# Reciprocals on another DMA queue, output chunks loaded two ahead, and the last block's closing steps behind later chunks, in a hybrid attention layer on one Trainium2 core

## The chip, the cores and the metric

The kernel runs on one core of one Trainium2 chip. The metric is device time in microseconds (us) of one execution. A core has TensorE (PE: matmuls, with PEld for its weight loads), VectorE (DVE), ScalarE (ACT), GpSimd (POOL) and SyncE (SP), each with an instruction queue of its own that it works through in order, and 16 DMA engines. Here SP issues nearly all DMAs. Three runs of the kernel before gave 1417.75 us in the median, 1410.29 to 1420.25.

## The reference

One encoder layer on 2048 positions of width 1024: an input projection, a gated linear attention over 512 of the columns, a softmax attention with 4 heads over the others, and one output projection with a residual and a LayerNorm. Only the last two stages bear on the change:

```python
    def attend(blk):
        qn, qr = blk
        s = (jnp.einsum('bqhd,bkhd->bhqk', qn, k_nope) + jnp.einsum('bqhr,bkr->bhqk', qr, k_r))
        p = jax.nn.softmax(s, axis=-1)
        return jnp.einsum('bhqk,bkhv->bqhv', p.astype(v.dtype), v)
...
    return jnp.concatenate([o_a, o_b], axis=-1) @ w_out
...
        x = layer_norm(DEEPNORM_ALPHA * x + mixed, ln_g[layer], ln_b[layer])
```

## The kernel before

Everything is float32. A matmul operand is split into a high part (`hi`, a copy to float32r on ACT, L115) and the rest (`lo`, a subtraction on DVE or POOL, L121), and a product is three matmuls (`mm3`, L147 to L149: high by high, low by high, high by low).

**Attention.** 16 blocks (4 heads by 4 groups of 512 queries). A block's scores come in 8 groups j of 256 keys: ten matmuls into a PSUM tile pS of two banks, of which there are two (L998 to L1002); `copy` on ACT takes it to a score tile s (L1007), `smax` on DVE keeps a running maximum (L1020). From the maxima come transposes on PE (mx, mb), then per group `sub` on DVE, `exp` on ACT, the split `phi` (ACT) and `plo` (POOL), the product `pv` with the values into a tile o, and the sums `acc`. The closing steps of a block are `tot` and `tsum` (the sums, transposed on PE into a tile sx in the bank pX), `rcp` (DVE: reduction L1108, reciprocal L1109, then the DMA of L1110 that stores 512 reciprocals to r_s in DRAM), `oh` and `ol` (split of o), `y` (the product with the value weights, into the bank pX) and `yc` (ACT copy, and the DMA of L1133 to ob_s). The queries of a later block are fetched by SP (L984, L988).

**Order.** All steps of the 16 blocks, and of the first four output chunks, are given a number, their place, in the tables PLACE, PLACE_LAST (for the last block) and PLACE_OUT. A place counts score groups: 8 to a block. `put` collects the steps; they are issued sorted by place, and `in_order` chains each engine's instructions, SP's too, in just this order. What comes behind that list (L1206 on) is ordered by the framework's scheduler, which goes by its own estimate of when each instruction is ready, and by program order where several are.

**Output chunks.** 16 chunks c of 128 positions. `load` (L1271) brings `of` (L1278: the linear attention's part; L1281: ob_s) and `gr` (L1279: the gates gm_s; L1280: the reciprocals r_s, broadcast). Both tiles come from the pool xf, which has two buffers in all. `gate` on POOL multiplies the second half of of by both parts of gr (L1287, twice), `hi` and `lo` split the halves. `product` is 48 matmuls per chunk, 24 for each half of the output columns, with `residual` on DVE after each half (L1331, then statistics L1332); even chunks write to the single banks pM and pX (pmb, px), odd ones to one tile of two banks (po). `finish` is the LayerNorm: L1344 to L1347, then `rsqrt` with Ln and Exp on ACT (L158, L159) and small DVE steps (L160 to L163), L1350, and two stores on SP (L1351). The rows of the output weights come by `fetch_w` (L1253) and are split into tiles woh and wol. `prepare(c)` loads and splits a chunk and loads its rows of x (xr, L1300). Chunks 0 to 3 are interleaved with the last block; for the others `prepare(c + 1)` stands ahead of chunk c's product. The last block's closing steps stand behind the finish of chunk 3.

Of the kernel before, what the change touches and what calls it, by code (L numbers as in the profile page):

```python
# [37 lines left out]
LATE_GATES = (NCH - 1, NCH - 2, 0)  # L38
STORE_POOL = (0, 1)
ENGINES = tuple(getattr(mybir.EngineType, n) for n in ("PE", "Activation", "DVE", "Pool", "SP"))  # L40
RND = 1.5 * 2.0 ** 23


# [28 lines left out]
PLACE_LAST = dict(  # L72
    sub=(9.1, 8.5, 8.63, 6.24, 10.95, 10.71, 7.9, 9.69),
    exp=(9.8, 11.1, 11.03, 11.51, 15.26, 10.75, 19.78, 16.58),
    hi=(11.57, 11.59, 12.49, 12.47, 16.56, 18.98, 23.59, 33.63),
    lo=(12.92, 14.95, 16.42, 18.28, 22.53, 23.3, 25.08, 34.29),
    pv=(15.43, 16.41, 17.68, 23.59, 30.52, 30.14, 33.06, 37.83),
    acc=(14.17, 13.67, 13.91, 12.97, 17.46, 24.17, 28.21, 33.8),
)


PRE_W, PRE_BLOCK = 4, 9
PLACE_OUT = dict(
    hi0=(-24.43, -15.24, -7.79, 34.96),
    lo0=(-21.2, -13.14, -5.7, 45.1),
    gate=(-19.0, -12.69, -4.28, 45.77),
    hi1=(-17.8, -11.53, 1.93, 46.3),
    lo1=(-16.64, -10.48, 17.64, 46.35),
    pre_hi=1.44,
    pre_lo=4.06,  # L90
    w_hi=0.11,
    w_step=5.72,
    w_lo=2.87,
    part=(0.52, 0.83, 3.02, 6.31, 9.13, 17.89, 18.98, 27.0),
    whole=(25.32, 49.8),
    sum=(41.6, 53.01),
)


# [7 lines left out]
class K:  # L107
# [20 lines left out]
        return s  # L128

    @contextmanager  # L130
    def in_order(self, last):


        traced = self.nc.cur_bb.bb.instructions
        end = traced[-1]
        yield
        n = next(k for k in reversed(range(len(traced))) if traced[k] is end) + 1
        for i in traced[n:]:
            if i.engine in ENGINES:
# [824 lines left out]
    def attention(self):  # L964
# [4 lines left out]
        with ExitStack() as ctx:  # L969
# [132 lines left out]

            def rcp(i):

                h, b = blocks[i]
                d = stt[i]
                rc = bp.tile([P, 4], F32, tag="rc", name=f"rc{i}")
                V.tensor_reduce(rc, d["x"], AX.X, ALU.add)  # L1108
                V.reciprocal(rc, rc)  # L1109
                nc.sync.dma_start(self.r_s[b][:, h].rearrange("o (e p) -> p (o e)", p=P), rc)  # L1110

            def oh(i):
                d = stt[i]
# [36 lines left out]
            def put(place, fn, *a):  # L1150
                todo.append((place, len(todo), fn, a))
# [5 lines left out]
            own = (("tot", tot), ("tsum", tsum), ("rcp", rcp), ("oh", oh), ("ol", ol), ("y", y), ("yc", yc))  # L1157
            for i in range(nb):
                for j in range(NP):
                    t = NP * i + j  # L1160
# [13 lines left out]
            for k in range(NK):  # L1174
                if k < PRE_W:
                    v = NP * (PRE_BLOCK + k)
                    hi, lo = v + out["pre_hi"], v + out["pre_lo"]
                else:
                    hi = end + out["w_hi"] + (k - PRE_W) * out["w_step"]
                    lo = hi + out["w_lo"]  # L1180
                if k == 0:
                    put(hi - 6, op.fetch_w, k)
                put(hi, op.split_hi, k)
                put(lo, op.split_lo, k)
                if k + 1 < NK:
                    put(lo + 0.01, op.fetch_w, k + 1)
                put(end + out["part"][k], lambda k: [op.part(o, k) for o in first[:2]], k)
            for c, o in enumerate(first):
                put(end + (out["lo1"][c - 1] + 0.01 if c else out["hi0"][0] - 6), op.load, o)
# [13 lines left out]
                    fn(*a)  # L1203
            ends = [i for e, i in last.items() if e not in (mybir.EngineType.PE, mybir.EngineType.DVE)]

            def prepare(c):  # L1206
                o = dict(c=c)
                with self.after(*ends):
                    op.load(o)
                    op.hi(o, 0)  # L1210
                    op.lo(o, 0)
                    op.gate(o)
                    op.hi(o, 1)
                    op.lo(o, 1)
                op.load_res(o)
                return o

            for o in first[:2]:
                op.finish(o)
            nxt = prepare(4)  # L1220
            for o in first[2:]:
                op.load_res(o)
                op.residual(o, 0)
                op.residual(o, 1)
                op.finish(o)
            with self.after(*last.values()):
                for _, f in own:
                    f(nb - 1)
            for c in range(4, NCH):
                o = nxt  # L1230
                if c < NCH - 1:
                    nxt = prepare(c + 1)
                op.product(o)
                op.finish(o)


class OutProj:
# [3 lines left out]
    def __init__(self, kern, ctx, qp, bp, sp, ps, pa, pb):  # L1241
        self.k, self.nc, self.qp, self.bp, self.sp, self.ps = kern, kern.nc, qp, bp, sp, ps
        self.single = (pa, "mb"), (pb, "x")
        self.sm = ctx.enter_context(kern.tc.tile_pool(name="smo", bufs=2, reuse_waits="tile"))
        self.raw, self.W = {}, {}
        self.ln = None

    def slot(self, name, dt=F32):
        return self.sp.tile([P, 2, 512], dt, tag="s", name=name)
# [15 lines left out]
    def split_lo(self, k):  # L1265
# [2 lines left out]
        self.k.lo(wl, self.raw[k], wh, "pool")  # L1268
        self.W[k] = wh, wl

    def load(self, o):  # L1271
# [9 lines left out]
        nc.sync.dma_start(of[:, 1], kern.ob_s[b][:, :, cs])  # L1281
        o["oh"], o["ol"] = [], []
# [51 lines left out]
    def finish(self, o):  # L1334
        kern, nc, sm = self.k, self.nc, self.sm
        V, Ac = nc.vector, nc.scalar
        c, rr = o["c"], o["rr"]
        if self.ln is None:
            self.ln = [self.slot(n) for n in ("lng", "lnb")]
            for t, n in zip(self.ln, ("ln_g", "ln_b")):  # L1340
                nc.sync.dma_start(t, kern.ins[n].rearrange("p (a d) -> p a d", a=2))
# [78 lines left out]
```

## Time and profile before

| What | us |
|---|---|
| median of three runs | 1417.75 |
| the profiled execution | 1418.9 |
| its span | 1417.1 |
| TensorE busy | 1318.7 |
| VectorE busy | 1006.3 |
| ScalarE busy | 823.6 |
| GpSimd busy | 730.1 |

Times in the profile are counted from the span's start. The projections and the linear attention take about the first half, attention reaches to about 1200 us, and the output chunks fill the rest, chunks 0 to 3 partly inside the last block. A timeline row gives start, duration, engine, line, operation, output from input, count, and in brackets the idle time of that engine just before, with what ended it. The chain of waits gives start, duration and what it was. Groups give busy time, mean ns and idle time. Matmuls are pipelined, so that one of 512 columns is shown as 0.39 us while the next starts 0.23 us later.

### The profile page before, as it was taken

The numbers are of one execution on the slowest core, as the hardware profiler recorded it, in microseconds if no ns is written. First come the engines' busy times: TensorE is split into PE (matmuls) and PEld (weight loads), VectorE is DVE, ScalarE is ACT, GpSimd is POOL, SyncE is SP. The second block draws the span as 40 slices with busy tenths as digits, with TensorE's granted clock in tenths as the row PEclk, the third lists the DMA queues.
The fourth block names the chain that finished last, engine by engine and source line by source line (L and its number), as shares of the span: only waits on it lengthen the run. The fifth ranks groups of instructions, "written<-read, shape, count | busy, mean of one in ns | idle before, by whom it ended". The sixth has DMA issues, their size and how long they took to land.

```text
span 1417.1 us, 19889 instructions
## 1 busy us (share of the span) xinstructions
PE 1318.7 (93%) x7056; PEld 1142.1 (81%) x7056; DVE 1006.3 (71%) x1829; ACT 823.6 (58%) x1353; POOL 730.1 (52%) x394
## 2 busy tenths in 40 slices
PE   6899999999989998899999999999999998966997
PEld 6899899998879888889788888888888776745785
DVE  7657754545687777776788888888888785564565
ACT  6555556555666555555688877888888685211100
POOL 3432423232332332330288888888899896634520
PEclk9899999999999999999999999999999999988999
DMA  7222223131655555544502332433332203565541
GB/s 248 75 67 69 72 62 108 53 86 57 208 196 172 171 172 161 183 154 135 156 1 38 45 43 45 64 46 66 52 82 38 68 15 43 197 159 176 176 158 45
DMA packets 108916, 147.39 MB, mean 104 GB/s; under 512 B 17838, under 2 KB 63278, under 8 KB 108816
## 3 DMA queue, kind: packets, MB, share of 16 engines
q1 hardware_dynamic: 108144, 144.02, 37.4%
q0 software_dynamic: 672, 2.10, 0.4%
q8 instruction: 56, 0.92, 0.3%
q14 instruction: 44, 0.36, 0.1%
HBM read 94.93 MB, written 51.15 MB: 103 GB/s over the span
## 4 chain that ended last, share of the span: by engine, by line
PE 46%; issue 6%; DVE 6%; DMA 6%; POOL 4%; ACT 4%; SPq 0%; DVEq 0%; POOLq 0%; ACTq 0%
PE o L148 4%; PE o L149 4%; PE o L147 4%; PE pS L998 4%; PE pS L1001 4%; PE pS L999 4%; PE pS L1000 4%; PE pS L1002 4%; DMA gr<-gm_s 2%; POOL of L1287 2%; PE po L147 1%; PE po L148 1%; PE po L149 1%; PE ipm L147 1%; DVE MMb L121 1%
## 5 line engine op out<-in xcount | busy, mean ns | idle before, releaser
L121 POOL TENSOR_TENSOR pl<-s,ph 128x1024 fp32r<-128x1024 f32 x128 | 306.2, 2410 | 61.3 <-ACT ph L115 46.7
L1020 DVE TENSOR_TENSOR rm<-pS,rm 128x512 f32<-128x512 f32 x210 | 144.5, 688 | 48.1 <-ACT s L1007 44.5
L1007 ACT ACTIVATE s<-pS 128x1024 f32<-128x1024 f32 x128 | 131.2, 1025 | 68.6 <-PE pS L1002 54.5
L1044 DVE TENSOR_TENSOR s<-s,mb 128x1024 f32<-128x1024 f32 x128 | 151.2, 1213 | 8.6 <-PE mb L1038 8.4
L115 ACT ACTIVATE ph<-s 128x1024 fp32r<-128x1024 f32 x128 | 133.8, 1058 | 26.8 <-PE o L149 26.1
L147 PE MATMUL ipa<-wah,xah 128*128 128x384 f32 (+1 forms) x384 | 131.6, 343 | 6.6 <-ACT wah L115 6.6
L1048 ACT ACTIVATE s<-s 128x1024 f32<-128x1024 f32 x128 | 132.7, 1049 | 8.3 <-DVE s L1044 6.0
L149 PE MATMUL ipa<-wah,xal 128*128 128x384 f32 (+1 forms) x384 | 126.7, 330 | 0.0
L148 PE MATMUL ipa<-wal,xah 128*128 128x384 f32 (+1 forms) x384 | 126.0, 328 | 0.0
L643 POOL TENSOR_TENSOR Us<-Us,cw 128x512 f32<-128x512 f32 x16 | 18.2, 1137 | 202.2 <-DVE Us L640 172.9
L998 PE MATMUL pS<-qh,ckvT_h 128*128 128x512 f32 x256 | 103.1, 403 | 1.9 <-ACT s L1007 1.3
L147 PE MATMUL o<-ph,vh 128*128 128x512 f32 x256 | 103.7, 405 | 0.1
L148 PE MATMUL o<-pl,vh 128*128 128x512 f32 x256 | 101.6, 397 | 1.9 <-POOL pl L121 1.9
L149 PE MATMUL o<-ph,vl 128*128 128x512 f32 x256 | 101.7, 397 | 0.0
L1001 PE MATMUL pS<-rh,krs 128*128 128x512 f32 x256 | 101.2, 395 | 0.0
L1000 PE MATMUL pS<-qh,ckvT_l 128*128 128x512 f32 x256 | 101.0, 395 | 0.0
L999 PE MATMUL pS<-ql,ckvT_h 128*128 128x512 f32 x256 | 101.0, 394 | 0.0
L1002 PE MATMUL pS<-rl,krs 128*128 128x512 f32 x256 | 100.8, 394 | 0.0
L1071 DVE TENSOR_TENSOR ap<-ap,s 128x512 f32<-128x512 f32 x120 | 83.5, 696 | 16.9 <-ACT s L1048 14.3
L115 ACT ACTIVATE oh<-of 128x512 fp32r<-128x512 f32 x32 | 20.2, 630 | 125.2 <-POOL of L1287 90.3
L147 PE MATMUL po<-woh,oh 128*128 128x512 f32 x144 | 59.7, 415 | 30.9 <-DVE rr L1331 27.8
L147 PEld LDWEIGHTS ipa<-wah,xah 128*128 128x128 f32 x384 | 74.3, 193 | 7.3 <-ACT wah L115 6.6
(319 smaller groups left out, 3938.0 us busy)
## 6 DMA issues: line engine op xcount, KB each, us to landing
xcf<-xT_dram SPq DMA_DIRECT2D x16, 512.0 KB, 4.6
xr<-x_dram SPq DMA_DIRECT2D x16, 512.0 KB
out_dram<-rr SPq DMA_DIRECT2D x32, 256.0 KB, 3.3
xaf<-xT_dram SPq DMA_DIRECT2D x14, 512.0 KB, 4.3
SU<-su_s SPq DMA_DIRECT2D x16, 256.0 KB, 4.5
qdb<-qd_s SPq DMA_DIRECT2D x16, 256.0 KB, 5.4
oib<-oi_s SPq DMA_DIRECT2D x16, 256.0 KB, 3.2
ub<-u_s SPq DMA_DIRECT2D x16, 256.0 KB, 3.5
```

The costliest lines, as they stand in the source:

```text
L115: return nc.scalar.activation(dst, src, AF.Copy).ins
L121: return e.tensor_tensor(dst, src, hi.bitcast(F32), ALU.subtract).ins
L147: mm(out, ah, bh, start=start, stop=False)
L148: mm(out, ah, bl, start=False, stop=False)
L149: mm(out, al, bh, start=False, stop=stop)
L998: mm(ps[:, e], kh, qh, start=True, stop=False)
L999: mm(ps[:, e], kh, ql, start=False, stop=False)
L1000: mm(ps[:, e], kl, qh, start=False, stop=False)
L1001: mm(ps[:, e], kr, rh, start=False, stop=False)
L1002: mm(ps[:, e], kr, rl, start=False, stop=True)
L1020: V.tensor_tensor(d["rm"], src[:, e], d["rm"], ALU.max)
L1044: V.tensor_tensor(s, s, d["mb"][:, None, :].to_broadcast([P, 2, QB]), ALU.subtract)
```

## The change

- `rcp` no longer issues a DMA. A new step `keep`, with a place of its own, issues the store of the reciprocals, now from ACT instead of SP.
- From chunk 4 on gr comes not from xf but from two tiles of the pool of score tiles, kept for even and odd chunks; xf then holds only the of tiles of these chunks.
- `load` and the split are taken apart: in chunk c's turn chunk c+2 is loaded and chunk c+1 is split. SP's instructions behind the list are chained in program order (`sp_order`).
- The last block's closing steps move from behind chunk 3's finish to behind the finishes of chunks 4 (tot, tsum), 5 (rcp, keep, oh, ol), 6 (y) and 7 (yc).
- The LayerNorm's two vectors are loaded in the list (`load_ln`), behind the split of the last weight rows, instead of at the first finish.
- All places are new.

```diff
 PLACE = dict(
-    copy=0.66,
-    max=0.98,
-    sub=(8.99, 8.91, 7.08, 8.85, 7.8, 5.4, 8.0, 7.24),
-    exp=(9.53, 10.02, 8.65, 9.56, 9.46, 9.27, 9.15, 8.24),
-    hi=(10.62, 10.59, 10.16, 10.6, 10.11, 10.96, 9.97, 10.3),
-    lo=(11.09, 12.25, 12.38, 11.97, 11.89, 11.89, 11.05, 10.44),
-    pv=(12.27, 12.73, 12.77, 12.49, 12.61, 12.3, 12.63, 11.92),
-    acc=(12.22, 11.24, 11.05, 0, 10.8, 11.32, 9.98, 9.11),
-    acc0=11.5,
-    tmax=1.41,
-    rmax=1.66,
-    bmax=1.67,
-    tot=10.0,
-    tsum=13.05,
-    rcp=15.73,
-    oh=12.61,
-    ol=12.89,
-    y=16.44,
-    yc=16.75,
+    copy=0.73,
+    max=1.21,
+    sub=(9.47, 8.65, 7.39, 7.37, 7.49, 6.63, 6.95, 7.44),
+    exp=(10.18, 9.95, 7.63, 9.15, 8.26, 9.12, 7.84, 8.01),
+    hi=(10.39, 10.41, 9.81, 10.32, 9.82, 10.74, 10.53, 10.47),
+    lo=(11.99, 11.22, 11.21, 12.62, 11.98, 11.51, 10.87, 10.63),
+    pv=(12.35, 12.1, 11.89, 12.65, 12.27, 12.25, 12.14, 11.45),
+    acc=(12.45, 11.78, 12.32, 0, 10.57, 11.24, 10.03, 9.22),
+    acc0=10.78,
+    tmax=1.26,
+    rmax=1.27,
+    bmax=1.48,
+    tot=11.2,
+    tsum=12.04,
+    rcp=13.55,
+    keep=14.21,
+    oh=12.34,
+    ol=12.99,
+    y=16.55,
+    yc=16.9,
 )
...
             def rcp(i):
-                h, b = blocks[i]
                 d = stt[i]
                 rc = bp.tile([P, 4], F32, tag="rc", name=f"rc{i}")
                 V.tensor_reduce(rc, d["x"], AX.X, ALU.add)
                 V.reciprocal(rc, rc)
-                nc.sync.dma_start(self.r_s[b][:, h].rearrange("o (e p) -> p (o e)", p=P), rc)
+                d["rc"] = rc
+
+            def keep(i):
+                h, b = blocks[i]
+                Ac.dma_start(self.r_s[b][:, h].rearrange("o (e p) -> p (o e)", p=P), stt[i]["rc"])
...
                 if k + 1 < NK:
                     put(lo + 0.01, op.fetch_w, k + 1)
+                else:
+                    put(max(lo, end + 26) + 0.02, op.load_ln)
...
-            def prepare(c):
-                o = dict(c=c)
-                with self.after(*ends):
-                    op.load(o)
-                    op.hi(o, 0)
-                    op.lo(o, 0)
-                    op.gate(o)
-                    op.hi(o, 1)
-                    op.lo(o, 1)
-                op.load_res(o)
-                return o
-
-            for o in first[:2]:
-                op.finish(o)
-            nxt = prepare(4)
-            for o in first[2:]:
-                op.load_res(o)
-                op.residual(o, 0)
-                op.residual(o, 1)
-                op.finish(o)
-            with self.after(*last.values()):
-                for _, f in own:
-                    f(nb - 1)
+            late = dict(last)
+            sp_order = lambda: self.in_order(late, SP_ONLY)
+            rest = {c: o for c, o in enumerate(first)}
+
+            def load(c):
+                if c < NCH:
+                    rest[c] = dict(c=c)
+                    op.load(rest[c])
+
+            def split(c):
+                if c < NCH:
+                    with self.after(*ends):
+                        for j in range(2):
+                            op.hi(rest[c], j)
+                            op.lo(rest[c], j)
+                            if j == 0:
+                                op.gate(rest[c])
+
+            with sp_order():
+                load(4)
+                for c in (2, 3):
+                    op.load_res(rest[c])
+                load(5)
+                for c in (0, 1):
+                    op.finish(rest[c])
+                split(4)
+                op.load_res(rest[4])
+                for c in (2, 3):
+                    op.residual(rest[c], 0)
+                    op.residual(rest[c], 1)
+                    op.finish(rest[c])
             for c in range(4, NCH):
-                o = nxt
-                if c < NCH - 1:
-                    nxt = prepare(c + 1)
-                op.product(o)
-                op.finish(o)
+                with sp_order():
+                    load(c + 2)
+                    split(c + 1)
+                    if c + 1 < NCH:
+                        op.load_res(rest[c + 1])
+                    op.product(rest[c])
+                    op.finish(rest[c])
+                with self.after(*last.values()), sp_order():
+                    for f in {4: (tot, tsum), 5: (rcp, keep, oh, ol), 6: (y,), 7: (yc,)}.get(c, ()):
+                        f(nb - 1)
...
-        gr = o["gr"] = kern.xfp.tile([P, 2, 4, P], F32, tag="xf", name=f"gr{c}")
+        if c < 4:
+            gr = kern.xfp.tile([P, 2, 4, P], F32, tag="xf", name=f"gr{c}")
+        else:
+            gr = self.gr[c % 2] = self.gr.get(c % 2) or self.slot(f"gr{c}").rearrange("p a (b d) -> p a b d", b=4)
+        o["gr"] = gr
```

The tables PLACE_LAST and PLACE_OUT have the same keys as before and new numbers.

More of the change, by code (lines that the diff above doesn't have):

```diff
@@ L40 @@
 ENGINES = tuple(getattr(mybir.EngineType, n) for n in ("PE", "Activation", "DVE", "Pool", "SP"))
+SP_ONLY = ENGINES[-1:]
 RND = 1.5 * 2.0 ** 23
@@ L51 @@
 PLACE = dict(
[L52 to L70 removed]
+    copy=0.73,
[18 more added lines that the diff above has]
+    yc=16.9,
 )
 PLACE_LAST = dict(
[L73 to L78, printed above, removed]
+    sub=(9.67, 8.74, 8.38, 6.77, 10.45, 3.53, 9.53, 5.55),
+    exp=(10.14, 9.35, 10.49, 8.31, 13.01, 14.59, 17.1, 18.05),
+    hi=(10.43, 11.83, 12.21, 14.39, 15.18, 22.96, 28.7, 34.03),
+    lo=(15.35, 16.07, 20.38, 20.41, 24.45, 25.82, 33.5, 36.25),
+    pv=(16.29, 16.53, 21.45, 24.62, 26.22, 30.32, 41.89, 43.83),
+    acc=(11.54, 13.81, 13.58, 13.82, 21.36, 25.57, 30.56, 39.92),
 )
@@ L83 @@
 PLACE_OUT = dict(
[L84 to L96, printed above, removed]
+    hi0=(-26.0, -16.05, -6.97, 34.17),
+    lo0=(-23.84, -12.96, -6.1, 40.96),
+    gate=(-20.72, -12.46, -4.41, 43.92),
+    hi1=(-19.28, -11.15, 1.03, 47.74),
+    lo1=(-16.82, -9.22, 22.19, 48.77),
+    pre_hi=1.22,
+    pre_lo=3.57,
+    w_hi=0.74,
+    w_step=6.49,
+    w_lo=4.26,
+    part=(1.05, 2.03, 5.45, 8.05, 10.24, 17.37, 21.96, 27.24),
+    whole=(24.99, 55.73),
+    sum=(38.16, 49.19),
 )
@@ L130, in in_order @@
     @contextmanager
-    def in_order(self, last):
+    def in_order(self, last, engines=None):
         traced = self.nc.cur_bb.bb.instructions
@@ L138, in in_order @@
         for i in traced[n:]:
-            if i.engine in ENGINES:
+            if i.engine in (engines or ENGINES):
                 if i.engine in last:
@@ L1155, in at @@
                 return p[j] if isinstance(p, tuple) else p
-            own = (("tot", tot), ("tsum", tsum), ("rcp", rcp), ("oh", oh), ("ol", ol), ("y", y), ("yc", yc))
+            own = (("tot", tot), ("tsum", tsum), ("rcp", rcp), ("keep", keep), ("oh", oh), ("ol", ol), ("y", y), ("yc", yc))
             for i in range(nb):
@@ L1269, in split_lo, with load_ln @@
         self.W[k] = wh, wl
+    def load_ln(self):
+        self.ln = [self.slot(n) for n in ("lng", "lnb")]
+        for t, n in zip(self.ln, ("ln_g", "ln_b")):
+            self.nc.sync.dma_start(t, self.k.ins[n].rearrange("p (a d) -> p a d", a=2))
     def load(self, o):
@@ L1337, in finish @@
         c, rr = o["c"], o["rr"]
[L1338 to L1341, printed above, removed]
         mv = sm.tile([P, 2], F32, tag="mv", name=f"mv{c}")
```

3 lines of the change are left out of this document (1 added, 2 removed).

## The prediction

> **What bounds the kernel now.** I read the page first, its busy times and slices; then a table of windows to see where TensorE is not full; then each engine's timeline in those windows, and SyncE's queue.
>
> ```profile
> PE 1318.7 (93%) x7056; PEld 1142.1 (81%) x7056; DVE 1006.3 (71%) x1829; ACT 823.6 (58%) x1353; POOL 730.1 (52%) x394
> 1000.00:1100.00 100.00, 100.00 (x451) 81.28 (x450) 84.36 (x115) 82.37 (x91) 91.83 (x42) 1.00 0.34 61
> 1180.00:1237.00 57.00, 52.22 (x221) 41.86 (x220) 29.80 (x48) 21.14 (x28) 36.64 (x20) 0.94 0.52 141
> 1237.00:1250.00 13.00, 8.77 (x34) 6.80 (x33) 12.83 (x27) 1.04 (x3) 4.40 (x3) 0.87 0.60 202
> 1250.00:1337.00 87.00, 59.96 (x245) 48.06 (x243) 45.52 (x80) 12.37 (x29) 40.26 (x30) 0.86 0.57 159
> 1337.00:1409.00 72.00, 70.76 (x308) 57.51 (x308) 40.35 (x87) 5.37 (x17) 15.72 (x12) 1.00 0.36 119
> ```
>
> In the window rows the columns are length, busy time (count) of PE, PEld, DVE, ACT and POOL, granted clock, DMA share and GB/s. Attention is bound by TensorE: 100 us busy in 100. So are the last output chunks, 70.76 in 72. Between them TensorE has holes, 4.2 us in 13 and 27 in 87, and the granted clock falls to 0.86: what it does run there runs partly at half speed. The timeline of PE names the holes; the bracket is the idle time before the row and what ended it.
>
> ```profile
> 1200.30 0.79 PE L147 MATMUL po<-woh,oh 128*128 128x512 f32 x1 [3.08 <-ACT woh L115]
> 1202.79 0.79 PE L148 MATMUL po<-wol,oh 128*128 128x512 f32 x1 [1.70 <-POOL wol L121]
> 1240.19 1.12 PE L1101 MATMUL sx<-ident,acc 128*128 128x128 f32 x4 [2.93 <-DVE rr L1331]
> 1249.63 0.50 PE L147 MATMUL y<-ofh,wv_h 128*128 128x512 f32 x1 [1.30 <-DVE u L1345]
> 1274.64 0.80 PE L147 MATMUL po<-woh,oh 128*128 128x512 f32 x1 [11.46 <-DVE rr L1331]
> 1310.46 0.80 PE L147 MATMUL po<-woh,oh 128*128 128x512 f32 x1 [13.29 <-DVE rr L1331]
> 1337.06 0.50 PE L147 MATMUL po<-woh,oh 128*128 128x512 f32 x1 [2.31 <-DVE rr L1331]
> 1402.87 0.50 PE L147 MATMUL po<-woh,oh 128*128 128x512 f32 x1 [0.78 <-DVE rr L1331]
> ```
>
> The hole of 11.46 us, followed backwards through ACT, POOL, DVE and SP:
>
> ```profile
> 1253.69 0.45 SPq L1133 DMA_DIRECT2D ob_s<-yc  x1
> 1254.66 0.52 SPq L1281 DMA_DIRECT2D of<-ob_s  x1
> 1267.35 2.60 POOL L1287 TENSOR_TENSOR of<-of,gr 128x512 f32<-128x512 f32 x2 [11.38 <-DMA of<-ob_s]
> 1269.98 0.63 ACT L115 ACTIVATE oh<-of 128x512 fp32r<-128x512 f32 x1 [15.66 <-POOL of L1287]
> 1270.52 0.19 ACT L158 ACTIVATE ln_l<-u 128x1 f32<-128x1 f32 x1
> 1270.97 0.99 DVE L160 TENSOR_TENSOR ln_t<-ln_y 128x1 f32<-128x1 f32 x1 [10.47 <-ACT ln_y L159]
> 1273.91 0.68 DVE L1331 SCALAR_TENSOR_TENSOR rr<-xr,po 128x512 f32<-128x512 f32 x1
> ```
>
> TensorE's second half of chunk 5 shares one tile with the first half and waits until DVE has added the residual to that (1273.91). DVE is in order and stood at chunk 4's LayerNorm (L160), whose Ln stood on ACT behind the split of chunk 6, which waited for the gate on POOL, which waited for a load issued at 1254.66. So a late load stops TensorE two chunks earlier, through three engines' queues. That load is late because both tiles of a chunk, of and gr, come from the two buffers of xf: it starts only when the chunk before is split. And the last block's two stores had just gone out on the same queue.
>
> **The change part by part.** First the chunk loop if no wait is left. TensorE has finished chunk 3 at 1240.19 - 2.93 = 1237.26. The pace of the full stretch, and the end:
>
> ```profile
> 1358.27 0.69 DVE L1331 SCALAR_TENSOR_TENSOR rr<-xr,po 128x512 f32<-128x512 f32 x1 [0.17 <-PE po L149]
> 1380.20 0.69 DVE L1331 SCALAR_TENSOR_TENSOR rr<-xr,po 128x512 f32<-128x512 f32 x1 [0.17 <-PE po L149]
> 1402.13 0.69 DVE L1331 SCALAR_TENSOR_TENSOR rr<-xr,po 128x512 f32<-128x512 f32 x1 [0.17 <-PE po L149]
> ```
>
> Two chunks take 21.93 us, one 10.97. From the start of chunk 4 to the first half of chunk 15 are 11.5 chunks, 126.1 us. The last block's four transposes and three matmuls stay as work, some 1.2 us (the rows of 1.12 and 0.50 were cold and first ones). From 1402.13 to the span's end at 1417.1 are 15.0 us, which the change leaves alone. 1237.3 + 126.1 + 1.2 + 15.0 = 1379.6 us: 37.5 less than the span. The holes from 1240 to 1337 sum to 31.3 us; the rest is the half clock behind them.
>
> *Loads two ahead.* In chunk c's turn SP now issues load(c+2), the residual's load, then chunk c's two stores. So load(c+3) stands behind the stores of chunk c, which wait for its LayerNorm. What that leaves:
>
> ```profile
> 1364.79 0.69 DVE L1331 SCALAR_TENSOR_TENSOR rr<-xr,po 128x512 f32<-128x512 f32 x1 [5.10 <-PE po L149]
> 1366.67 0.20 ACT L158 ACTIVATE ln_l<-u 128x1 f32<-128x1 f32 x1 [3.91 <-DVE u L1345]
> 1369.42 1.00 SPq L1351 DMA_DIRECT2D out_dram<-rr  x2
> gr<-r_s SPq DMA_DIRECT2D x16, 256.0 KB, 5.0
> of<-ob_s SPq DMA_DIRECT2D x16, 256.0 KB, 6.2
> ```
>
> The product ended at 1364.62, 0.17 before the first row; the stores leave 4.8 to 5.8 us after that. Four loads take 2.1 us to issue (0.52 each as at 1254.66), 5.0 to 6.2 to land; then one gate multiply (1.3, half of POOL's 2.60), hi (0.63) and lo (1.3). Together 16 to 17 us, and two products give 21.9: 5 us to spare, so TensorE doesn't wait for a split. The two gate tiles come out of the pool of score tiles, whose last two are free once block 15 is summed; nothing waits for that.
>
> What can be late next is ACT's order, which is the scheduler's here. Ln of chunk c+1 is ready 2.05 us into product c+2 (1366.67). The split's hi of chunk c+3 is ready 5.8 + 2.1 + 5.0 to 6.2 + 1.3 = 14.2 to 15.4 us into product c+1, which is 3.2 to 4.4 into product c+2. If it stands first, Ln waits 1.2 to 2.4 us more, the stores and the next loads go out that much later, and this repeats. In the trace above the split of chunk 6 stood ahead of Ln of chunk 4, so it can. Bounds over the nine turns in which this can happen: 0, and 9 x 2.4 = 22. I take 2, near the low end, since ahead of it stand loads 4 and 5, which come early.
>
> *Closing steps* between chunks 4 and 7: sx and y use the x bank that even chunks use too. Each has a whole odd chunk of room; I take 1 us for TensorE standing before one of them, between 0 and the 1.30 it stood at y.
>
> *Reciprocals on ACT's queue.* The store, and what came behind it in two places:
>
> ```profile
> 1184.98 0.37 SPq L1110 DMA_DIRECT2D r_s<-rc  x1
> 1188.97 14.12 SPq L1253 DMA_DIRECT2D wof<-wO_dram  x2
> 1188.97 10.19 DMA wof<-wO_dram
> wof<-wO_dram SPq DMA_DIRECT2D x8, 512.0 KB, 4.4
> 1252.98 0.61 SPq L1110 DMA_DIRECT2D r_s<-rc  x1
> ```
>
> 512 values of 4 bytes each go to DRAM. The weight load 4 us behind it took 10.19 us against a median of 4.4; the chunk load at 1254.66 took 12.7 (its gate began at 1267.35) against 6.2. So a store of 2 KB costs the transfers behind it about 6 us. Whether it is the queue or the memory, the trace can't show: all these transfers are on SP's queue. I take it that they stay slow, so the holes of 3.08 and 1.70 us at 1200 remain, and the last block's store, now in product 5, eats the 5 us to spare of load 7: 0 to 5 us of hole, I take 2. The Trainium skill's page "DMA: Bandwidth & Descriptors", section "Issuing engines are not separate DMA queues", says the same against this part: DMAs of all issuing engines interleave on the same 16 DMA engines, and another issuer saves issue time alone. No row here shows an ACT-issued transfer.
>
> On ACT the issue itself is bounded by SP's 0.37 and 0.61 us, in 16 blocks.
>
> ```profile
> L1007 ACT ACTIVATE s<-pS 128x1024 f32<-128x1024 f32 x128 | 131.2, 1025 | 68.6 <-PE pS L1002 54.5
> L1020 DVE TENSOR_TENSOR rm<-pS,rm 128x512 f32<-128x512 f32 x210 | 144.5, 688 | 48.1 <-ACT s L1007 44.5
> 1184.06 0.68 DVE L1108 TENSOR_REDUCE rc<-sx 128x4 f32<-128x512 f32 x1
> 1184.78 0.18 DVE L1109 RECIPROCAL rc<-rc 128x4 f32<-128x4 f32 x1
> ```
>
> The score copies wait 54.5 us for TensorE in 16 blocks, 3.4 a block: that covers it. Were the cover gone, 16 x 0.61 = 10 us.
>
> *The new places.* Sorted by place within a block's period of eight, POOL's order within a block is the old one; DVE and ACT change some subtractions and exponentials with maxima and copies; on PE the sums' transposes go one score group earlier and the third product ahead of a score group. With TensorE full there is nothing to win, and no place puts a consumer ahead of its producer: 0, bounds -3 (the idle of the window 1180:1237 is 4.8) and +8 (0.5 a block).
>
> The sum: 1379.6 + 2 + 1 + 2 = 1384.6 us of span. The profiled execution took 1418.9 for 1417.1 of span, and the median is 1417.75: 1384.6 + 1.8 - 1.15 = 1385 us, 2.3% less.
>
> **The rivals.** *Stores gate loads.* ACT's order puts the splits first throughout: 11 to 22 us instead of 2, 1394 to 1405 us. For it the row at 1269.98; against it, Ln is the earlier one in program order.
>
> *The queue was the cause.* On a queue of its own the 4-byte store delays nobody: the 4.8 us of holes at 1200 and about 2 of half clock go, and the 2 us in product 5: 1376. Against it: gm_s of the same chunk, issued before the store, was slow too.
>
> ```profile
> 1252.41 10.07 DMA gr<-gm_s
> ```
>
> *The holes only move.* The hole of 13.29 at 1310 comes again in another chunk, since the scheduler still orders ACT and DVE by its own times: 1385 + 13 and its half clock, 1400 to 1412, within 1% above 1403.6.
>
> *ACT stands at the store (slower).* ACT is in order; keep waits there for the reciprocal, and the score copies behind it hold the two pS banks, so TensorE stops in each block. At most DVE still has a max pair (1.38), an add (0.70, as L1020's), the reduction (0.68) and the reciprocal (0.18) to do: 2.9, with the issue 3.5 us. If none of it is covered, 15 x 3.5 = 52: 1437. It decides from 2.2 us a block, where 15 x 2.2 eats the gain. Against it: keep lies two thirds of a group (2.6 us) behind rcp, and the 3.4 us of cover.
>
> **How the numbers follow.** Forecast 0.50; stores gate loads 0.17; own queue 0.12; holes move 0.14, half of it beyond 1403.6; ACT stands 0.07. About 1%, 14 us, is what a measurement can tell here: faster is below 1403.6, slower above 1431.9. Faster 0.50 + 0.17 + 0.12 + 0.07, less 0.05 for the gating's upper end: 0.81; same 0.12; slower 0.07. The range reaches from the queue's case (1374) to the gating and half the moved holes (1405); outside are the rest of these and ACT's case, under 0.2.
>
> **What would show it.** Right: PE near 100% busy from chunk 4 on, pace 10.97 a chunk, chunk loads issued before the chunk ahead is split, the row of 3.08 at 1200 still there. Gating: Ln late behind a hi of a chunk two ahead, stores drifting later each turn. Own queue: wof lands in under 5 us behind keep. ACT: idle on PE before pS in every block. The forecast is wrong if a hole over 5 us remains in chunks 4 to 15, or if the attention window falls below 99 in 100.

## The result and the profile after

| | before | after |
|---|---|---|
| median, us | 1416.11 (1410.29 to 1420.25, 4 runs) | 1400.69 (1396.22 to 1402.29, 4 runs) |
| the profiled execution, us | 1418.9 | 1396.22 |
| its span, us | 1417.1 | 1394.4 |
| ratio of the times | | 0.9889, 95% interval 0.9846 to 0.9932 |

The change saves 15.4 us between the medians, 22.7 us between the two profiled executions: the profiled one of after is the fastest of its four. Everything worked out below from rows stands against the span of 1394.4 us.

The windows of after, cut as in the prediction; columns are length, then busy time (count) of PE, PEld, DVE, ACT and POOL, granted clock, DMA share, GB/s:

```profile
1000.00:1100.00 100.00, 100.00 (x452) 81.30 (x451) 83.81 (x113) 83.06 (x90) 92.00 (x42) 1.00 0.26 68
1180.00:1237.00 57.00, 54.12 (x229) 43.62 (x228) 32.43 (x57) 17.29 (x26) 39.89 (x23) 0.97 0.55 158
1237.00:1250.00 13.00, 11.31 (x53) 9.08 (x51) 12.74 (x34) 1.45 (x5) 1.07 (x1) 1.00 0.50 159
1250.00:1337.00 87.00, 75.59 (x310) 60.35 (x309) 48.71 (x87) 11.20 (x27) 36.69 (x29) 0.94 0.57 170
```

Attention is as full as it was. Between 1250 and 1337 us TensorE is busy 75.6 us in place of 60.0, and the clock is 0.94 in place of 0.86. The timeline of PE in after, all rows from 1180 us on with more than 0.5 us of idle time ahead of them:

```profile
1194.73 0.50 PE L150 MATMUL po<-wol,oh 128*128 128x512 f32 x1 [0.79 <-POOL wol L123]
1229.78 0.47 PE L149 MATMUL pmb<-woh,oh 128*128 128x512 f32 x1 [2.09 <-DVE rr L1360]
1245.15 0.66 PE L1103 MATMUL sx<-ident,acc 128*128 128x128 f32 x4 [1.69 <-DVE rr L1360]
1259.79 0.80 PE L149 MATMUL po<-woh,oh 128*128 128x512 f32 x1 [6.65 <-DVE rr L1360]
1284.32 0.50 PE L149 MATMUL po<-woh,oh 128*128 128x512 f32 x1 [0.84 <-DVE rr L1360]
1308.65 0.50 PE L149 MATMUL po<-woh,oh 128*128 128x512 f32 x1 [2.27 <-DVE rr L1360]
1333.99 0.50 PE L149 MATMUL po<-woh,oh 128*128 128x512 f32 x1 [1.65 <-DVE rr L1360]
1357.80 0.50 PE L149 MATMUL po<-woh,oh 128*128 128x512 f32 x1 [1.74 <-DVE rr L1360]
1380.16 0.50 PE L149 MATMUL po<-woh,oh 128*128 128x512 f32 x1 [1.20 <-DVE rr L1360]
```

The holes of 11.46 and 13.29 us are gone. One of 6.65 us is left, and a smaller one ahead of the second half of every odd chunk, each ended by a residual (L1360 here, L1331 before). Those rows stand 24.53, 24.33, 25.34, 23.81 and 22.36 us apart, where two chunks took 21.93 us in the full stretch of before. Both kinds have to be explained. First the 6.65 us, in after's timelines of ACT and SP and then in its chain of waits (start, duration, what it was):

```profile
1246.77 0.40 ACTq L1115 DMA_DIRECT2D r_s<-rc  x1
1247.20 0.69 SPq L1329 DMA_DIRECT2D xr<-x_dram  x1
```
```profile
1247.20 11.71 DMA xr<-x_dram
1259.04 0.70 DVE rr L1360
1259.79 0.80 PE po L149
```

The store of the last block's reciprocals leaves on ACT's queue; 0.4 us later SP issues the rows of x of chunk 5, and these take 11.71 us where the median in this trace is 5.5. DVE cannot add the residual of the first half without them, and TensorE cannot start the second.

### The profile page after: what moved, and what is told of

Same layout as the page of the kernel before. It is cut to its first block, busy times and chain, and to the rows that moved or that the text cites. A ratio compares the mean times of both kernels' runs of the same rounds, so it can differ in the third digit from the quotient of the medians.

```text
span 1394.4 us, 19845 instructions
## 1 busy us (share of the span) xinstructions
PE 1318.6 (95%) x7056; PEld 1141.4 (82%) x7056; DVE 1012.8 (73%) x1829; ACT 825.9 (59%) x1353; POOL 725.1 (52%) x394
## 4 chain that ended last, share of the span: by engine, by line
PE 44%; DVE 12%; DMA 6%; ACT 3%; issue 2%; SPq 1%; POOL 1%; DVEq 0%; POOLq 0%; ACTq 0%
PE o L149 4%; PE o L150 4%; PE o L151 4%; PE pS L1000 4%; PE pS L1003 4%; PE pS L1002 4%; PE pS L1004 4%; PE pS L1001 4%; DMA xr<-x_dram 2%; DVE MMb L123 2%; DMA of<-ob_s 1%; PE po L149 1%; PE po L150 1%; PE ipm L149 1%; PE po L151 1%
## 5 line engine op out<-in xcount | busy, mean ns | idle before, releaser
L151 PE MATMUL ipa<-wah,xal 128*128 128x384 f32 (+1 forms) x384 | 126.1, 328 | 0.0
L150 PEld LDWEIGHTS ipa<-wal,xah 128*128 128x128 f32 x384 | 74.0, 193 | 1.3 <-DVE wal L123 0.6
```

The costliest lines, as they stand in the source:

```text
L150: mm(out, ah, bl, start=False, stop=False)
L151: mm(out, al, bh, start=False, stop=stop)
```

## The experiments

### The queue of the store

One line of `keep`: `Ac.dma_start` becomes `nc.sync.dma_start`; everything else is as in after.

> The changed kernel with one part undone: the reciprocals are stored through SP's queue again, in the same place of the order. Theory (the cost is in the 4-byte writes, whatever queue they come from): within 4 us of the changed kernel's 1400 us, since the transfers behind the store are slow either way; the hole of about 6.7 us in the fifth chunk stays. Rival (the queue was the cause): 5 to 15 us slower than the changed kernel, the weight load behind block 14's store lands in 10 us again and the hole at the weights comes back.

1402.22 us (1398.44 to 1407.87), ratio to before 0.9909, 0.9875 to 0.9943; after has 0.9889. No difference is measured between the two queues, as the theory said. But the hole moves with the store: chunk 5 keeps 1.41 us of it. The store is issued at 1270.63 here, and the rows of x that SP issues 2.9 us behind it take 14.4 us; a wait of 7.24 us stands at the split of another chunk (PE's timeline):

```profile
1283.92 0.80 PE L149 MATMUL pmb<-woh,oh 128*128 128x512 f32 x1 [7.24 <-ACT oh L117]
```

### The form of the store

The same 2 KB a block, from four partitions of 128 values in a row instead of 128 partitions of 4 single values. This kernel leaves out the right reciprocals; it stores other values in their place:

```diff
+            wide = bp.tile([P, P], F32, name="wide", bufs=1)
+            V.tensor_copy(wide, self.ident)
...
-                V.reciprocal(rc, rc)
+                V.reciprocal(wide[:, 0:4], rc)
...
-                Ac.dma_start(self.r_s[b][:, h].rearrange("o (e p) -> p (o e)", p=P), stt[i]["rc"])
+                nc.scalar.dma_start(self.r_s[b][0, h].rearrange("(e p) -> e p", p=P), wide[0:4])
```

> The changed kernel, storing the same 2 KB from ACT's queue at the same place but as four rows of 512 bytes instead of 512 values of 4 bytes. What it stores is a tile that holds the reciprocals of the first positions in its first four columns and an identity elsewhere, so the gates multiply by other values. Theory (4-byte writes slow all transfers for some 8 to 12 us): the hole of 6.65 us goes with its half clock, the weight loads land in under 5 us, 8 to 12 us faster than the changed kernel: 1388 to 1392. Rival (it is the stall of the queue or the place of the closing steps): no more than 3 us.

1391.28 us (1383.6 to 1393.13), ratio 0.9819, 0.9784 to 0.9853: 9.4 us below after in the medians. Its profiled execution is the fastest of its four, 1383.6 us with 1381.8 of span, so the rows show the good end of its runs. In them the two holes behind a store are gone: PE has no idle time over 0.3 us between 1180 and 1224 us, and none at the second half of chunk 5. The rows of x of chunk 5, issued 0.43 us behind the store, are there 6.05 us later, where after waits for them 11.71 (the timelines of SP and DVE):

```profile
1243.34 0.77 SPq L1331 DMA_DIRECT2D xr<-x_dram  x1
```
```profile
1249.39 0.69 DVE L1362 SCALAR_TENSOR_TENSOR rr<-xr,po 128x512 f32<-128x512 f32 x1 [1.87 <-DMA xr<-x_dram]
```

The size of a write (4 or 512 bytes) and their number (512 or 4) change together here, and no run separates them.

The small holes ahead of the odd chunks' second halves stay, and their pace of some 24 us too (PE's timeline):

```profile
1273.26 0.50 PE L149 MATMUL po<-woh,oh 128*128 128x512 f32 x1 [1.61 <-DVE rr L1362]
1297.38 0.50 PE L149 MATMUL po<-woh,oh 128*128 128x512 f32 x1 [2.07 <-DVE rr L1362]
```

So the two kinds of hole have different causes. Most of the sections that follow look for the second.

### The order of ACT

Behind the list ACT follows the scheduler's order in after, and there the hi of chunk c+2 stands right ahead of the Ln of chunk c. Here ACT goes in program order:

```diff
-SP_ONLY = ENGINES[-1:]
+SP_ONLY = (ENGINES[1], ENGINES[-1])
```

> The changed kernel with ACT's instructions behind the list chained in program order, as SP's are, so that the LayerNorm of chunk c stands ahead of the split of chunk c+2. Theory (that order couples stores, loads and LayerNorm): the holes of 1.2 to 2.3 us in chunks 9 to 15 go back to 0.8 or less and two chunks take 21.9 us instead of 22.4 to 25.3; 6 to 10 us faster, 1390 to 1394. Rival (DVE's work or the landing of the loads sets the pace): within 3 us of the changed kernel.

1403.29 us (1399.65 to 1404.02), ratio 0.9915, 0.9891 to 0.994. No gain: the theory falls in this form. TensorE now stands elsewhere. In after as here it runs the first matmuls of the next even chunk, c+3, ahead of the second half of the odd chunk c+2, and here these stand for the split of c+3 (PE's timeline, then the chain of waits):

```profile
1307.09 0.51 PE L151 MATMUL pmb<-woh,ol 128*128 128x512 f32 x1 [3.60 <-POOL ol L123]
1334.00 0.50 PE L151 MATMUL pmb<-woh,ol 128*128 128x512 f32 x1 [3.20 <-POOL ol L123]
```
```profile
1294.08 0.75 DVE rr L1375
1296.80 0.62 SPq L1309
1297.46 5.61 DMA of<-ob_s
...
1305.77 1.28 POOL ol L123
```

Two chunks take 26.9 us. The chain begins at the LayerNorm of chunk c (L1375) and goes over its stores to the load of c+3. So the stores do gate loads, whatever ACT's order.

### The place of the closing steps

All of the last block's closing steps stand ahead of chunk 4, as in before, and the loop is the new one:

```diff
+            with self.after(*last.values()), sp_order():
+                for _, f in own:
+                    f(nb - 1)
...
-                    for f in {4: (tot, tsum), 5: (rcp, keep, oh, ol), 6: (y,), 7: (yc,)}.get(c, ()):
-                        f(nb - 1)
```

> The changed kernel with the last block's closing steps back in front of chunk 4, all other parts kept. Theory (with loads two ahead, the place of the closing steps moves the slow stretch of transfers and two short waits, no more): within 5 us of the changed kernel. Rival (moving the closing steps is what removed the holes of 11.5 and 13.3 us): 10 us slower or more, about 1410.

1396.79 us (1395.6 to 1399.36), ratio 0.987, 0.9847 to 0.9893: within the range of after, as the theory said. Spreading these steps over four chunks bought nothing that can be measured.

### The stores a turn later

SP issues the two stores of chunk c behind the load and the rows of x of the next turn, so that these no longer wait for chunk c's LayerNorm:

```diff
                     if c > 4:
+                        op.out(rest[c - 1])
...
-                    op.finish(rest[c])
+                    op.finish(rest[c], False)
```

> The changed kernel; from chunk 4 on a chunk's two output stores stand one turn later in SP's order, behind the next loads and rows of x, all else kept. Theory (loads and rows of x wait on SP behind stores that wait for the LayerNorm, and so DVE's residual and TensorE's second half wait for rows of x): two chunks take 21.9 to 22.2 us from chunk 8 on instead of 22.4 to 25.3, no wait of DVE for xr, 6 to 10 us faster than the changed kernel, 1391 to 1395. Rival (the loads themselves land too late because all transfers of a chunk share the DMA engines): within 3 us of it.

1397.29 us (1392.26 to 1399.64), ratio 0.9882, 0.9852 to 0.9913. That is 3.4 us below after, with ranges that overlap: less than the theory's 6 to 10. The waits of DVE from 1237 to 1390 us say what came in place of the rows of x (line waited for, us in total, times, longest):

```profile
DVE rr L1364 <- DMA xr<-x_dram: 10.3, 1, 10.3
DVE ln_t L162 <- ACT ln_y L161: 9.0, 5, 2.2
```

The one wait for xr is the one behind the 4-byte store. The other five are DVE's LayerNorm waiting for ACT's Ln.

The same with the reciprocals of the last two blocks stored in rows of 512 bytes, transposed on PE and copied by ACT:

> The run before plus the reciprocals of the last two blocks turned on TensorE (one transpose each, copied by ACT) and stored as four rows of 512 bytes; the output is the reference's. Theory: both gains add up, 9 us from the store as in the run with rows and 6 to 10 from the order: 1382 to 1386, no hole over 3 us behind 1200. Rival: they remove the same idle time, 1389 to 1393.

1393.51 us (1389.92 to 1396.31), ratio 0.9852, 0.9822 to 0.9882: 3.8 us less than without the rows, where the rows brought 9.4 us to after. DVE still waits 8.7 us for ln_y. The rival is nearer.

### Both orders at once

Stores a turn later and ACT in program order; then the same with the last reciprocals in rows.

> The changed kernel with both edges of the suspected loop broken at once: the stores of chunk c issued a turn later on SP, behind the load and the rows of x, and ACT's work in program order, so that the hi copies of chunk c+2 no longer stand ahead of the Ln of chunk c. Alone the first gave 1397.3 us and the second 1403.3 us against 1400.7 us. Theory (either edge alone keeps the loop closed: with the stores moved the loop runs by ACT's order, with ACT's order changed it runs by the stores): with both gone no wait of an odd chunk is left, two chunks take 21.9 to 22.4 us in place of 22.4 to 25.3 us, and the four pairs behind 1284 us save 5 to 8 us; the hole of the 4-byte store stays: 1391 to 1395 us. Rival (the chunks are held by the transfers themselves, whatever the order): two chunks take 23 us or more, 1396 to 1401 us.

1405.64 us (1404.32 to 1406.49), ratio 0.9899, 0.9878 to 0.9921.

> As the kernel with the stores a turn later and the last reciprocals written in rows of 512 bytes (1393.5 us), with ACT's work in program order besides. The theory of the two edges: no wait over 2 us from 1200 us on, two chunks in 21.9 to 22.4 us, 1382 to 1388 us. Rival (the transfers hold the chunks): 1391 to 1396 us, no different from the same kernel without ACT's program order.

1401.55 us (1398.94 to 1404.89), ratio 0.9873, 0.9849 to 0.9898. The theory of two edges falls, and neither time lies in the range of its rival: each is some 8 us slower than with the stores' move alone. From one split of an even chunk to the next two chunks take 29.1 us in the first (1335.44 to 1364.51) and 28.5 in the second (1330.09 to 1358.59). The chain of waits of the second:

```profile
1317.66 0.75 DVE rr L1394
1320.04 0.61 SPq L1320
1320.70 5.34 DMA of<-ob_s
1326.21 1.27 POOL of L1327
...
1328.77 1.27 POOL ol L123
1330.09 0.80 PE pmb L151
```

It is the chain of the stores again. The LayerNorm of an odd chunk, 9 here, ends more than a turn late. Its store, though a turn later on SP, is waited for by the load of chunk 13, and the gate of that chunk stands on POOL ahead of the split of chunk 12 that TensorE needs.

### The same stores without their wait

The stores keep their place on SP and their bytes, but read the LayerNorm's factors, which are always there:

```diff
+            src = rr if c < 2 or c == NCH - 1 else self.ln[0]
-            nc.sync.dma_start(kern.out[c * P:(c + 1) * P, n * 512:(n + 1) * 512], rr[:, n])
+            nc.sync.dma_start(kern.out[c * P:(c + 1) * P, n * 512:(n + 1) * 512], src[:, n])
```

In this kernel the scheduler puts a split even between the Ln and the Exp of one LayerNorm on ACT: DVE waits 5.25 us for it once, ahead of 1269.58 us.

> The changed kernel in which the stores of the chunks from 2 to the last but one keep their place on SP and their bytes, but read the tile of the LayerNorm's factors, which has stood there since long before: the traffic is the same, and no store waits for a LayerNorm (those chunks of the output hold the factors). Theory (the waits of the stores on SP, ahead of the loads and the rows of x, are what the odd chunks lose): two chunks take 21.9 to 22.4 us in place of 22.4 to 25.3 us, the waits of the second halves for the rows of x go, and with the hole of the 4-byte store still there it is 1390 to 1395 us. Rival (the transfers' own time under this traffic holds the chunks, so that three orders have changed nothing): two chunks take 23 us or more, 1397 to 1402 us.

1394.1 us (1391.7 to 1395.28), ratio 0.985, 0.9831 to 0.9869: 6.6 us below after, as the theory said. The pace only comes late. The residuals of the first halves of chunks 9, 11 and 13, on DVE:

```profile
1308.08 0.68 DVE L1360 SCALAR_TENSOR_TENSOR rr<-xr,po 128x512 f32<-128x512 f32 x1
...
1331.02 0.68 DVE L1360 SCALAR_TENSOR_TENSOR rr<-xr,po 128x512 f32<-128x512 f32 x1
...
1352.95 0.69 DVE L1360 SCALAR_TENSOR_TENSOR rr<-xr,po 128x512 f32<-128x512 f32 x1 [0.17 <-PE po L151]
```

From chunk 5 to 7 it is 30.30 us, with the wait of 5.25 in it, then 23.14 and 22.94, and 21.93 in the last two pairs. At 1308.08 and 1331.02 there is no bracket: DVE came to the residual from other work, without waiting for anything.

> As the kernel whose stores don't wait, with the reciprocals of all blocks written in rows of 512 bytes from a tile of the identity as in the kernel of 1391.3 us (other values, so the output of the second branch is off): both suspected costs gone. Theory (the 4-byte store and the waits of the stores are the whole difference to the sum of the prediction, 1379.6 us of span without waits): no wait over 3 us behind 1200 us, two chunks in 21.9 to 22.4 us, 1381 to 1386 us. Rival (something else holds the chunks): 1388 to 1392 us, no different from the rows alone.

1393.27 us (1390.96 to 1395.2), ratio 0.9851, 0.9829 to 0.9872. The theory that the store and the stores' waits are everything falls: with both gone it is not measurably faster than with one. Writing the reciprocals in rows was worth 9.4 us in after, 3.8 with the stores a turn later and 0.8 here (for the last two blocks alone in the second case): its price depends on what else is late. And a hole of 4.43 us still stands ahead of chunk 5's second half with both suspects gone (PE, then DVE):

```profile
1256.67 0.79 PE L149 MATMUL po<-woh,oh 128*128 128x512 f32 x1 [4.43 <-DVE rr L1362]
```
```profile
1246.25 3.26 DVE L1374 SCALAR_TENSOR_TENSOR rr<-rr,mv,lng 128x512 f32<-128x512 f32 x2
...
1252.67 3.35 DVE L1377 SCALAR_TENSOR_TENSOR rr<-rr,ln_r,lnb 128x512 f32<-128x512 f32 x2
```

From 1246.25 to the residual at 1255.94 DVE waits 0.47 us for another engine. But these two pairs, 1.41 and 1.42 us elsewhere, are more than twice as long here. So there is a third limit, on DVE itself.

### Places and loop apart

Before with all new places and nothing else, then after with the old places and the store on SP where it was.

> The kernel before with the three new tables of places alone; the store stays on SP in rcp's place, the chunk loop is the old one. Theory (the places gave the 7 to 9 us by which chunk 4 starts earlier; the chunk loop keeps its two holes): 1408 to 1413, chunk 4 starts at about 1230 us instead of 1237 or 1241. Rival (the places gave nothing, the earlier start comes from ACT's queue or the new order on SP): 1414 to 1420.

1420.76 us (1413.19 to 1426.72, 10 runs), ratio 1.004, 1.002 to 1.0061. The places alone cost 5 us instead of saving some. The profiled execution is the fastest of the ten, 1413.19 us, so its rows show one cost and not the sum. The 4-byte store is at work again (SP, ACT and PE):

```profile
1175.15 0.37 SPq L1111 DMA_DIRECT2D r_s<-rc  x1
1175.62 0.45 SPq L1254 DMA_DIRECT2D wof<-wO_dram  x1
...
1188.23 1.06 ACT L116 ACTIVATE woh<-wof 128x1024 fp32r<-128x1024 f32 x1 [11.80 <-DMA wof<-wO_dram]
...
1194.14 0.80 PE L149 MATMUL o<-pl,vh 128*128 128x512 f32 x1 [8.77 <-POOL pl L122]
```

At its new place the store of `rcp` comes right ahead of a load of weights. ACT, and POOL behind it, stand in order at the split of these weights, and TensorE waits 8.77 us for a score split that is queued behind. In after, where the store is a step of its own, 5.2 us lie between the two (1178.17 and 1183.38).

> The changed kernel with the old tables of places and the store on SP in the reciprocal's place: the new chunk loop alone. Theory (the loop takes away the holes of 11.5 and 13.3 us and brings in the slower pace): 1403 to 1409. Rival (the loop gains nothing without the new places): 1414 or more.

1407.82 us (1402.47 to 1410.16, 9 runs), ratio 0.995, 0.9934 to 0.9966: 7.5 us of gain for the loop alone, as the theory said. Minus 7.5 and plus 5.4 do not make the 15 us of both together. In these runs the places pay only together with `keep` and the new loop; which of the two they need was not tried.

## Why the prediction was right in sign and 10 us off in the sum

The forecast was 1385 us, 1373 to 1405. The time came out 15.7 us above the forecast and inside the range, and the change saves 15.4 us where 32.8 were forecast. Its sum for the span was 1384.6 us, and the span of the profiled execution, the fastest of the four, is 1394.4. Where the 9.8 us lie:

| term | in the sum | in the trace of after |
|---|---|---|
| TensorE has finished chunk 3 | 1237.3 | 1229.78 - 2.09 = 1227.7 |
| to the residual of the first half of chunk 15 | 126.1 + 1.2 + 5 of waits = 132.3 | 1379.4 - 1227.7 = 151.7 |
| from there to the end | 15.0 | 15.0 |

The middle row alone is 19.4 us over the sum, and 9.6 us that the sum did not have, ahead of the loop, hide half of it. Without them the time would, by estimate, be about 1410 us, outside the range: that it lies inside is in part luck. The prediction's own signs say so too. A hole over 5 us remains in chunk 5, the pace is not 10.97 us a chunk, and the row of 3.08 us at 1200 is not there.

**Chunk 3 ends 9.6 us earlier, not at the same time.** I had kept the holes at 1200 us, since the store would still slow the weights. It does, but from another place: 0.79 us of hole is left of 3.08 and 1.70, which is 4.0 us, and the clock behind them stays up (0.97 in the window from 1180, 0.94 before), by estimate 0.03 of 57 us, 1.7 us more. Those two are 5.7 of the 9.6; the rest was not taken apart. The last block's matmuls of scores also end earlier, at 1161.1 in place of 1164.8, but the new places reorder PE's work there, so that it is no measure of a gain. I had put 0 for the places, with -3 and +8 as bounds.

**The rival of the queue was rightly held to be small.** On SP the store costs what it costs on ACT, within what the runs can tell. The rows of the trace had only shown that whatever came behind it was slow; the run with rows says that it is the form of the write, in four rows or in 512 values.

**The store was mis-sized.** "0 to 5 us of hole, I take 2" counted load 7 and its 5 us to spare. What the store hit was xr of chunk 5, which is issued just behind it and has no such room: 6.65 us of hole, and the clock falls to 0.86 between 1250 and 1275 us. From chunk 3's end to the first residual of chunk 5 after takes 31.4 us, and 1.5 chunks are 16.5: 14.9 us over. In the kernel with rows the same way takes 25.0 us (1224.4 to 1249.4), 6.4 less. The other 8.5 us are not the store's. 3.8 of them in after, and 4.8 in the kernel with rows, are holes ahead of chunk 4 and ahead of the closing transposes, which end with a residual on DVE; the rest was not taken apart. The prediction's window from 1237 had DVE at 12.83 us of 13 there.

**The step that failed is the pace.** "Two chunks take 21.93 us, one 10.97" was read from the last three odd chunks of before and applied to all. I wrote "TensorE doesn't wait for a split", which held in after, and looked for what could be late on ACT and SP. I had shown the limit and passed over it: the residuals at 1358.27, 1380.20 and 1402.13 each have 0.17 us of idle time ahead of them. Behind the even chunk's second residual that is DVE's whole reserve. DVE works in order, and the residual of the odd chunk's first half stands behind the even chunk's LayerNorm. DVE's timeline of before, in that stretch:

```profile
1374.76 0.69 DVE L1331 SCALAR_TENSOR_TENSOR rr<-xr,px 128x512 f32<-128x512 f32 x1 [3.38 <-PE px L149]
...
1376.52 1.41 DVE L1347 SCALAR_TENSOR_TENSOR rr<-rr,mv,lng 128x512 f32<-128x512 f32 x2
1377.85 0.16 DVE L160 TENSOR_TENSOR ln_t<-ln_y 128x1 f32<-128x1 f32 x1
...
1378.62 1.42 DVE L1350 SCALAR_TENSOR_TENSOR rr<-rr,ln_r,lnb 128x512 f32<-128x512 f32 x2
```

From the second residual of one odd chunk to the first residual of the next, TensorE needs 15.41 us (1364.79 to 1380.20). DVE works 15.41 - 3.38 - 0.17 = 11.86 of them. Its 3.38 us of idle time lie ahead of the even chunk's second residual; behind that only 0.17 are left. Now the same stretch of after, DVE first, then POOL:

```profile
1290.10 0.69 DVE L1360 SCALAR_TENSOR_TENSOR rr<-xr,po 128x512 f32<-128x512 f32 x1 [5.10 <-PE po L151]
...
1291.87 3.19 DVE L1372 SCALAR_TENSOR_TENSOR rr<-rr,mv,lng 128x512 f32<-128x512 f32 x2
1295.53 1.03 DVE L162 TENSOR_TENSOR ln_t<-ln_y 128x1 f32<-128x1 f32 x1 [0.47 <-ACT ln_y L161]
...
1303.56 1.03 DVE L162 TENSOR_TENSOR ln_t<-ln_y 128x1 f32<-128x1 f32 x1 [0.32 <-ACT ln_y L161]
...
1307.91 0.69 DVE L1360 SCALAR_TENSOR_TENSOR rr<-xr,po 128x512 f32<-128x512 f32 x1 [1.29 <-issue]
```
```profile
1291.53 2.98 POOL L1316 TENSOR_TENSOR of<-of,gr 128x512 f32<-128x512 f32 x2 [2.63 <-DMA of<-ob_s]
1295.25 1.29 POOL L123 TENSOR_TENSOR ol<-of,oh 128x512 fp32r<-128x512 f32 x1 [0.74 <-ACT oh L117]
1303.28 1.29 POOL L123 TENSOR_TENSOR ol<-of,oh 128x512 fp32r<-128x512 f32 x1 [6.74 <-ACT ln_l L160]
```

A step on one column, 0.16 us in the rows of before, takes 1.03 us twice, and ends within 0.02 us of the POOL instruction beside it (1296.56 and 1296.54; 1304.59 and 1304.57). The pair of L1372 takes 3.19 us for 1.41. The residual, which reads one of its inputs from PSUM, is not lengthened: 0.69 us at 1283.58, with POOL's gates running from 1281.74 to 1284.77. The prediction had shown such a step too and read it as a wait alone: 0.99 us for L160 at 1270.97, ending with POOL's split beside it (1271.96 and 1271.95 in the trace). The Trainium skill says of this, on the page "SBUF — State Buffer", section "SBUF: two separate sides", that DVE and GpSimd share one pair of ports as an exclusive lock, which a DVE operation with two SBUF inputs also needs, and that the loser is blocked for the other's whole instruction. These ends agree with it, to 0.02 us.

So POOL's gates and splits, which in before were done beside the holes, now fall on every pair of chunks. POOL is busy 36.7 of the 87 us from 1250 in after; in the 72 us of before that gave the pace it is busy 15.7, all of them by 1366. Between an odd chunk's second and the next one's first residual after takes 15.7, 17.8, 17.2, 17.3 and 15.8 us in the five pairs from 1267.91 on, 6.8 us over five times 15.41. Not all of that is POOL's: right ahead of two of these residuals DVE also waits, 0.90 us for rows of x and 1.29 us for something that the profile does not name. The product that follows, 6.52 us at full clock, takes 8.87 and 8.15 us behind the two largest holes, 4.0 over; 2.35 of these follow the hole of the 4-byte store. That is the 10.7 us that the pairs are above 21.93, where the sum had 3 for gating and for the closing steps.

The kernel whose stores don't wait shows it most plainly. From 1291.45 to 1308.08, 16.63 us, DVE shows no idle time; its five lengthened steps, 2.54, 1.25, 2.45, 1.78 and 1.24 us against 1.41, 0.16, 1.42, 1.41 and 0.16, add 4.7 to the 11.86 us. The first 3.55 us of that use up the idle time of before, and the 1.15 left are close to what the stretch loses: 16.63 - 15.41 = 1.22. The kernel with both suspects gone gives the same sum with other numbers. From 1288.38 to 1307.01, again without idle time, seven lengthened steps add 6.92 us; 3.37 are left over, and the stretch is 3.22 over 15.41. That is why freeing the transfers alone gained little: where a wait for one went, DVE's work was just behind it. The rival "stores gate loads" was real, and 6.6 us by this run, between the 2 that I took and the 11 that I gave it as a case of its own. From chunk 7 on the pairs of that run take 5.9 us less than those of after. Little of it went through ACT's order in after: DVE's four waits for ln_y from 1237 to 1390 us add up to 3.4 us, and ACT in program order gained nothing. What the runs show is SP's order: the rows of x, which I had not counted behind load(c+2) and for which DVE waits 4.5 us in the kernel with rows, and in two other orders the load of a later chunk.

That DVE beside POOL holds the pairs is read from rows of these kernels and from these sums; no run of its own took POOL's work away, or set the first residual of an odd chunk ahead of the even chunk's LayerNorm. The nearest to it lies inside the traces. In the two kernels whose stores don't wait, POOL's last instruction ends at 1341.2 and 1340.4 us, and the pairs from chunk 11 on take the 21.93 us of the prediction (21.92 once). The loads of chunks have ended there too, so this alone would not tell the two apart. Why the fastest and the median of the kernel with 512-byte rows lie 7.7 us apart stays open.

**The other steps.** Attention stayed at 100 in 100. ACT did not stand at the store: its issue took 0.37 to 0.40 us. "The holes only move" gave 1400 to 1412 us for a hole of 13 us. One of 6.65 did come, in chunk 5, behind the store.

## What to carry to other kernels

Before a pace is carried from one stretch to another, look at the smallest idle time in it, not at the busy share: 0.17 us ahead of a residual was all the reserve at that place, and it was measured where another engine had stopped working. A transfer's price is asked by the form of its writes and by what is issued in the microseconds behind it, on either of the two queues tried here. And when changes of order gain little or nothing, the next suspect is an engine that goes from one to the next without idling.

## What the runs showed of the hardware

- 512 single values of 4 bytes written to DRAM slow what is issued in the following microseconds, on the same queue or another: rows of x took 11.71 us against a median of 5.5 with the store on ACT and the load on SP, and 14.4 with both on SP. Behind the same 2 KB as four rows of 512 bytes they were there in 6.05 us.
- DVE steps with two tensor inputs from SBUF stand still beside a POOL tensor operation, even one column wide: 1.03 to 1.25 us against 0.16. A step of 512 columns with one input from PSUM kept its 0.69 us.
